# Decoder layer with retrieved experts: low halves of weights on VectorE, scores evicted together with their maximum, one-hots of 16 tokens, retrieval by heads, two u loads ahead of the gates' load

## The chip, the cores and the metric

The program runs on one core of a Trainium2 chip, in one launch. The metric is the device time of one execution in microseconds (us). The core has a matrix engine (TensorE, PE in the profile, with its weight loads as PEld), VectorE (DVE), ScalarE (ACT), GpSimd (POOL) and a queue that issues most DMAs (SP). Every engine works through its own instructions in a fixed order and waits on semaphores for the others.

## The reference

One layer over 16 meta tokens and 512 tokens of width 1024; float32 in and out.

```python
h = layer_norm(concat([meta, x]))
q, k, v, gb, gc, z = split(h @ w_in)                 # w_in: 1024 x 3072
attn = softmax(q1 k1 / 8 + bias) v - lam * softmax(q2 k2 / 8 + bias) v   # 4 heads, causal, T5 bias
conv = gb * short_conv(gc * z)                       # width 3, causal
h = layer_norm(ALPHA * h + concat([norm(attn), conv]) @ w_out)
# PEER: 8 heads, 2 x 128 sub-keys, 16384 experts
s = (h @ w_q) . sub_keys                             # per token: 8 heads x 2 x 128 scores
s1, i1 = top16(s[..., 0, :]); s2, i2 = top16(s[..., 1, :])
sc, ci = top16(s1[:, None] + s2[None, :])
idx = i1[ci // 16] * 128 + i2[ci % 16]; g = softmax(sc)
out = sum over the 128 experts of a token:  g * gelu(h . u[idx]) * v[idx]
return layer_norm(ALPHA * h + out)[16:]
```

## The kernel before

Float32 operands are split into a float16 high half (made by ScalarE) and a low half (made by VectorE), and each product is three float16 matmuls (`mm3`, line 145). `split` (line 105) does that for u and v rows, for projections and for most weights. `load_w` loads one block of 512 weight columns in four pieces `w` (four buffers) and splits them into `wh` and `wl`, of which there are three buffers. For the blocks gc, z, gb and w_out two of the four pieces go through `split_pool`, in which ScalarE scales the piece in place and rounds it, and GpSimd makes the low half.

The code is written in the order of the layer, and a scheduler of the tile framework fixes the order of each engine's instructions from it, within the limits of the tile buffers.

1. Up to about 320 us: layer norm, projections, and 16 attention units (4 blocks of 128 queries `i`, 4 heads `h`). `att_a` multiplies queries with keys, VectorE evicts the two score tiles with scale and bias (L348), takes the row maximum over both (L352), and ScalarE takes the exponential. `att_t`, `att_b` and `att_c` transpose, multiply with v and normalise; `rstd` does the reciprocal square root on GpSimd. Convolution and output projection (`conv_gc` and the others) are put between the units.
2. About 320 to 440 us: queries of the retrieval (`pq_mm`), scores with the sub-keys, and `top16` on VectorE, in four rounds of two heads; a round multiplies the queries of both its heads, then their scores, then ranks them.
3. About 440 to 717 us: 56 u blocks (of 128 that cover all experts) are multiplied with the tokens of blocks 1 to 3 by `u_first`; the first `NSP` results go to memory (`ascr`), the other `NR` stay on the chip. Between them the generator `finish_topk` is advanced by a budget (`SIDE` per block against the numbers it yields): it ranks the candidates of a block of tokens, retrieves expert numbers by a comparison and a multiplication (`soh`, L598 to L604), and, for blocks 1 to 3, builds for `TB` tokens at a time one-hot tiles (L664 to L667), which TensorE multiplies to a gate matrix (`expand`). The matrices go through memory: GpSimd's queue writes `gscr`, SP's queue loads `gr`.
4. From 717 us: for each of the 128 blocks a product gate times activation `w` (L821) and 18 matmuls with v (L831). The 72 blocks that are left get their u product one step ahead (`prep`). Token block 0 is served by 128 gathers (`g_issue`, `g_dot`, `g_acc`) in VectorE's spare time.

Of the kernel before, what the change touches and what calls it, by code (L numbers as in the profile page):

```python
# [16 lines left out]
P = 128  # L17
# [22 lines left out]
TB = 8  # L40
# [3 lines left out]
NSP = 36  # L44
NR = 20
# [7 lines left out]
def build(tc, A, out):  # L53
# [72 lines left out]
    def split_pool(hi, lo, src, scale):  # L126
        S.activation(src, src, AF.Copy, scale=scale)
        S.activation(hi, src, AF.Copy)
        G.tensor_tensor(lo, src, hi, op=OP.subtract)

    def load_w(src, nb, pool=False):
        wh = wst.tile([P, KT, 512], F16, name="wh")
        wl = wst.tile([P, KT, 512], F16, name="wl")
        for j in range(4):
            w = wst.tile([P, 2, 512], F32, name="w", bufs=4)
            s = slice(j * 2, j * 2 + 2)
            SY.dma_start(w, src[nb, :, s, :])
            (split_pool if pool and j % 2 else split)(wh[:, s, :], wl[:, s, :], w, WS)
        return wh, wl
# [17 lines left out]
    with ExitStack() as s1:  # L157
# [92 lines left out]
        for c0, c1 in ((0, 512), (512, RW)):  # L250
            p = bank()
            PE.matmul(p[:H, :c1 - c0], rb, oh[:, c0:c1], start=True, stop=True)
            S.copy(row[:, c0:c1], p[:H, :c1 - c0])
# [34 lines left out]
        def conv_gc(c):  # L288
            if c == 0:
                W["gc"] = load_w(A["w_in"], 4, True)  # L290
# [3 lines left out]
        def conv_z(c):  # L294
            if c == 0:
                W["z"] = load_w(A["w_in"], 5, True)
# [4 lines left out]
        def conv_gb(c):  # L301
            if c == 0:
                W["gb"] = load_w(A["w_in"], 3, True)
# [8 lines left out]
        def out_proj(i, nb):  # L312
            for b in range(2):
                if ("wo", b) not in W:
                    W["wo", b] = load_w(A["w_out"], b, True)
# [19 lines left out]
        def att_a(i, h):  # L335
# [3 lines left out]
            qs = slice(i * P, (i + 1) * P)  # L339
            rs_ = [slice(m * DK, (m + 1) * DK) for m in range(2)]  # L340
# [173 lines left out]

    with ExitStack() as s5:
# [7 lines left out]
        for nb in range(4):  # L523
            if nb < 3:
                wqs[nb + 1] = load_w(A["w_q"], nb + 1)
            w = wqs.pop(nb)
            if nb == 0:
                pq = pq0
            else:
                pq = [None] * 4  # L530
                pq_mm(w, pq, 0, 512)
            todo = []
            for hh in range(2):
                h = nb * 2 + hh
                pqh = kp.tile([P, 2, T], F16, name="pqh", bufs=2)
                pql = kp.tile([P, 2, T], F16, name="pql", bufs=2)
                for j in range(2):
                    split(pqh[:, j, :], pql[:, j, :], pq[2 * hh + j], 1.0 / WS)
                for i in range(NT):
                    ts = slice(i * P, (i + 1) * P)  # L540
                    p = bankA()
                    for j in range(2):
                        mm3(p[:, j * NK:(j + 1) * NK], lambda k: pqh[:, j, ts], lambda k: pql[:, j, ts],
                            lambda k: keyh[:, h, j, :], lambda k: keyl[:, h, j, :], 1)
                    sc = kp.tile([P, 2, NK], F32, name="sc", bufs=8)
                    S.activation(sc, p[:, :2 * NK].rearrange("p (j n) -> p j n", j=2), AF.Copy,
                                 scale=1.0 / WS)
                    todo.append((h, i, sc))
            for n, (h, i, sc) in enumerate(todo):
                if nb == 3 and n % 3 == 0:  # L550
                    u_first(n // 3)
# [351 lines left out]
```

## Time and profile before

| | |
|---|---|
| median of 3 runs | 1530.44 us (1519.59 to 1531.7) |
| profiled execution | 1525.47 us; span of the trace 1523.7 us |
| mean granted TensorE clock | 0.968 |
| busy: PE, DVE, ACT, POOL | 92%, 80%, 48%, 20% of the span |
| DMA | 370.90 MB, 243 GB/s over the span |

The times are those of whole executions. The profile is of one execution; its span begins with the first instruction, so the 1.8 us between its two numbers lie around the span. A busy share is an average over the four stages, which have different limits.

### The profile page before, as it was taken

Reading aid. Unit: us, or ns where it says so; the run is one execution under the profiler, and the core shown is the slowest. Engines: PE = TensorE matmul, PEld = TensorE weight load, DVE = VectorE, ACT = ScalarE, POOL = GpSimd, SP = SyncE. Lnnn points to the kernel's source line nnn. Section 1 sums busy time; section 2 is a strip of 40 time slices with the busy share of each in tenths; the row PEclk is TensorE's granted clock in tenths of the full one; section 3 lists DMA queues with packets and bytes.
Section 4 is the critical chain, followed back from the end, with each engine's and each line's share of the span. In section 5 each row is a group of like instructions: output and inputs, shape, how many; then the busy total and the mean of one; then the engine's idle time right before and its main releaser. Section 6 shows DMA issues by size and latency. Waiting matters only on the chain.

```text
span 1523.7 us, 22893 instructions
## 1 busy us (share of the span) xinstructions
PE 1399.8 (92%) x8656; PEld 760.9 (50%) x8656; DVE 1224.3 (80%) x2375; ACT 730.2 (48%) x1243; POOL 299.8 (20%) x288
## 2 busy tenths in 40 slices
PE   6889897889989889897999999999999999999993
PEld 2345455554546556573554545545454545554551
DVE  8454687479999999894797897878978797888785
ACT  5364455351337658484454444444445444444441
POOL 2031111110001313011123232212212222212214
PEclk9989998989999999998999999999999999999997
DMA  6452110060055848589898998989989999999851
GB/s 231 146 176 76 57 56 1 30 208 15 2 171 180 262 140 272 186 237 365 333 365 337 355 378 337 374 341 338 403 319 360 357 348 352 362 352 366 298 197 56
DMA packets 85987, 370.90 MB, mean 243 GB/s; under 512 B 10495, under 2 KB 15647, under 8 KB 69492
## 3 DMA queue, kind: packets, MB, share of 16 engines
q1 hardware_dynamic: 57724, 200.53, 36.0%
q0 software_dynamic: 28144, 168.90, 30.1%
q8 instruction: 67, 1.10, 0.3%
q14 instruction: 44, 0.36, 0.1%
q10 hardware_dynamic: 8, 0.01, 0.0%
HBM read 335.05 MB, written 35.69 MB: 243 GB/s over the span
## 4 chain that ended last, share of the span: by engine, by line
PE 46%; issue 19%; DVE 19%; DMA 6%; POOL 6%; ACT 3%; POOLq 0%; SPq 0%; DVEq 0%; ACTq 0%
PE po L831 21%; PE pa L145 12%; PE b L145 11%; POOL grow L686 3%; DMA grow<-peer_uv,idx 2%; DVE ul L107 2%; DVE wl L107 1%; DMA gscr<-stg 1%; DVE rh L666 1%; DVE rl L667 1%; DVE oh L664 1%; DMA w<-w_in 1%; DVE oh L665 1%; DMA kf<-keysT 1%; POOL ry L83 1%
## 5 line engine op out<-in xcount | busy, mean ns | idle before, releaser
L145 PE MATMUL pa<-tTh,uh 128*128 128x384 f16 x1024 | 336.0, 328 | 10.3 <-ACT act L499 9.9
L145 PE MATMUL pa<-tTh,ul 128*128 128x384 f16 x1024 | 335.8, 328 | 9.0 <-DVE ul L107 9.0
L145 PE MATMUL pa<-tTl,uh 128*128 128x384 f16 x1024 | 335.9, 328 | 0.0
L686 POOL DMA_INDIRECT grow<-peer_uv,idx x128 | 169.9, 1328 | 615.8 <-DVE acc L703 552.4
L145 PEld LDWEIGHTS <-uh 128*128 128x128 f16 x2048 | 200.2, 98 | 148.4 <-issue 13.9
L831 PEld LDWEIGHTS <-wwh 128*128 128x128 f16 x1488 | 145.8, 98 | 181.2 <-ACT wwh L823 12.0
L107 DVE SCALAR_TENSOR_TENSOR ul<-uf,uh 128x1024 f16<-128x1024 f32 x128 | 161.5, 1262 | 90.9 <-ACT uh L106 90.9
L106 ACT ACTIVATE uh<-uf 128x1024 f16<-128x1024 f32 x128 | 135.2, 1056 | 198.1 <-PE pa L145 192.3
L831 PE MATMUL po<-pvh,wwh 128*128 128x512 f16 x744 | 182.1, 381 | 10.9 <-ACT pvh L106 10.4
L831 PE MATMUL po<-pvl,wwh 128*128 128x512 f16 x744 | 181.8, 381 | 0.0
L831 PE MATMUL po<-pvh,wwl 128*128 128x512 f16 x744 | 180.8, 379 | 0.0
L107 DVE SCALAR_TENSOR_TENSOR pvl<-vf,pvh 128x1024 f16<-128x1024 f32 x128 | 155.6, 1219 | 26.4 <-ACT pvh L106 26.4
L106 ACT ACTIVATE pvh<-vf 128x1024 f16<-128x1024 f32 x128 | 134.3, 1050 | 70.4 <-PE po L831 70.2
L703 DVE SCALAR_TENSOR_TENSOR acc<-grow,gact,acc 128x1024 f32<-128x1024 f32 x127 | 162.5, 1279 | 0.6 <-ACT gact L695 0.6
L693 DVE SCALAR_TENSOR_TENSOR grow<-grow,x 128x1024 f32<-128x1024 f32 x128 | 156.1, 1219 | 7.6 <-DMA grow<-peer_uv,idx 7.4
L145 PEld LDWEIGHTS <-ul 128*128 128x128 f16 x1024 | 100.8, 98 | 78.0 <-DVE ul L107 11.4
L823 ACT ACTIVATE wwh<-w 128x384 f16<-128x384 f32 x128 | 66.7, 522 | 145.3 <-DVE w L821 145.3
L145 PE MATMUL b<-tTh,wh 128*128 128x512 f16 (+4 forms) x416 | 123.6, 322 | 0.9 <-ACT tTh L124 0.9
L145 PE MATMUL b<-tTl,wh 128*128 128x512 f16 (+4 forms) x416 | 124.0, 320 | 0.0
L145 PE MATMUL b<-tTh,wl 128*128 128x512 f16 (+4 forms) x416 | 123.8, 320 | 0.0
L831 PEld LDWEIGHTS <-wwl 128*128 128x128 f16 x744 | 72.8, 98 | 87.8 <-issue 0.2
L145 PEld LDWEIGHTS <-wh 128*128 128x128 f16 x832 | 70.3, 100 | 63.7 <-issue 4.3
(229 smaller groups left out, 1911.3 us busy)
## 6 DMA issues: line engine op xcount, KB each, us to landing
uf<-uT SPq DMA_DIRECT2D x128, 512.0 KB, 6.5
vf<-vL SPq DMA_DIRECT2D x128, 512.0 KB, 7.3
gscr<-stg POOLq DMA_DIRECT2D x12, 2048.0 KB, 12.4
gr<-gscr SPq DMA_DIRECT2D x32, 768.0 KB, 8.1
w<-w_in SPq DMA_DIRECT2D x24, 512.0 KB, 4.8
w<-w_q SPq DMA_DIRECT2D x16, 512.0 KB, 4.1
ascr<-act POOLq DMA_DIRECT2D x18, 384.0 KB, 4.8
aload<-ascr SPq DMA_DIRECT2D x18, 384.0 KB, 8.9
```

Of the source, the lines that this page charges most:

```text
L83: G.tensor_tensor(y[:n], ve[:n], mhalf[:n].to_broadcast([n, w]), op=OP.pow)
L106: S.activation(hi, src, AF.Copy, scale=scale)
L107: V.scalar_tensor_tensor(lo, src, scale, hi, op0=OP.mult, op1=OP.subtract)
L145: m = PE.matmul(o, a(k), b(k), start=first and n == 0, stop=last and n == 3 * nk - 1)
L664: V.tensor_tensor(pairs(o2), row, mid(gT[:, 1, ts]), op=OP.is_equal)
L665: V.tensor_tensor(pairs(o1), row, mid(gT[:, 0, ts]), op=OP.is_equal)
L666: V.tensor_tensor(pairs(rh), pairs(o2), mid(gT[:, 2, ts]), op=OP.mult)
L686: G.indirect_dma_start(out=uv, out_offset=None, in_=A["peer_uv"], in_offset=bass.IndirectOffsetOnAxis(ap=idx[:, j:j + 1], axis=0))
L693: V.scalar_tensor_tensor(uv[:, :D], uv[:, :D], 1.0, x1[0], op0=OP.mult, op1=OP.mult, accum_out=c)
L703: V.scalar_tensor_tensor(acc, uv[:, D:], c, acc, op0=OP.mult, op1=OP.add)
L823: S.activation(wh, w, AF.Copy)
L831: PE.matmul(po[i][c], x[:, ts], y[:, c * 512:(c + 1) * 512], start=f and k == 0, stop=False)
```

## The change

- `split_pool` is gone: all pieces of all weights go through `split`.
- `att_a` evicts a score tile with one instruction that also keeps the running minimum of the negated score. The bias is stored eight times larger, the exponential gets the scale -1, and the separate maximum is gone.
- The retrieval's queries, scores and ranking run in eight rounds of one head; the queries of the next head are multiplied ahead of the scores of the present one. The three u products among them stand at other places.
- In `finish_topk` the expert numbers are stored in pairs, the multiplication of the retrieval reads them in pairs, and all eight of them run on VectorE (four ran on GpSimd).
- One-hots are built for 16 tokens at a time, in two buffers (three before), and expanded one group behind (two before).
- 40 of the 56 early u results go to memory (36 before), 16 stay (20 before). The u loads and splits of the first two later blocks are written ahead of the first load of gates.

```diff
-TB = 8
+TB = 16
-NSP = 36
-NR = 20
+NSP = 40
+NR = 16
...
-            (split_pool if pool and j % 2 else split)(wh[:, s, :], wl[:, s, :], w, WS)
+            split(wh[:, s, :], wl[:, s, :], w, WS)
...
-                    V.scalar_tensor_tensor(lg[:, m, f0:f1], p[:, :f1 - f0], DK ** -0.5,
-                                           bias[h][:, c0 + f0:c0 + f1], op0=OP.mult, op1=OP.add)
-            nm = small.tile([P, 2], F32, name="nm")
+                    V.tensor_tensor_reduce(lg[:, m, f0:f1], p[:, :f1 - f0], bias[h][:, c0 + f0:c0 + f1],
+                                           scale=-DK ** -0.5, scalar=nm[:, m:m + 1] if f0 else 3.0e38,
+                                           op0=OP.add, op1=OP.min, accum_out=nm[:, m:m + 1])
-            V.tensor_reduce(nm, lg[:, :, :w], axis=AX.X, op=OP.max, negate=True)
             for m in range(2):
                 S.activation(lg[:, m, :w], lg[:, m, :w], AF.Exp, bias=nm[:, m:m + 1],
-                             accum_out=z[:, m:m + 1])
+                             scale=-1.0, accum_out=z[:, m:m + 1])
...
+        def pq_head(h):
+            nb, hh = divmod(h, 2)
+            if hh == 0 and nb < 3:
                 wqs[nb + 1] = load_w(A["w_q"], nb + 1)
             if nb == 0:
+                return pq0[2 * hh:2 * hh + 2]
+            pq = [None] * 4
+            pq_mm(wqs[nb], pq, 0, 512, (2 * hh, 2 * hh + 1))
+            return pq[2 * hh:2 * hh + 2]
+
+        nxt = pq_head(0)
+        for h in range(PH):
+            pq = nxt
...
+            if h + 1 < PH:
+                nxt = pq_head(h + 1)
...
-        V.tensor_copy(ivh, iv[i])
+        for j in range(2):
+            V.tensor_copy(ivh[:, j], iv[i][:, :, j, :].unsqueeze(3).to_broadcast([P, PH, K, 2]))
...
-            (V if i <= 1 else G).tensor_tensor(
-                o, o, ivh[:, :, j, :].unsqueeze(3).to_broadcast([P, PH, K, K]), op=OP.mult)
+            o2 = o.rearrange("p h a (m e) -> p (h a) m e", e=2)
+            V.tensor_tensor(o2, o2, ivh[:, j].rearrange("p h a e -> p (h a) e").unsqueeze(2)
+                            .to_broadcast([P, PH * K, K // 2, 2]), op=OP.mult)
...
-                o1 = tkp.tile([P, TB, NK], F16, name="oh1", bufs=3)
-                o2 = tkp.tile([P, TB, NK], F16, name="oh2", bufs=2)
-                rh = tkp.tile([P, TB, NK], F16, name="rh", bufs=3)
-                rl = tkp.tile([P, TB, NK], F16, name="rl", bufs=3)
+                o1 = tkp.tile([P, TB, NK], F16, name="oh1", bufs=2)
+                o2 = tkp.tile([P, TB, NK], F16, name="oh2")
+                rh = tkp.tile([P, TB, NK], F16, name="rh", bufs=2)
+                rl = tkp.tile([P, TB, NK], F16, name="rl", bufs=2)
...
-                yield 1.8
-                if len(prev) == 2:
+                yield 3.2
+                if len(prev) == 1:
                     flush()
...
+    for n1 in [n for n in seq if n >= NSP + NR][:2]:
+        u_load(n1)
     load_g(0)
```

The scheduler's order changes in two places that matter below. The first is VectorE ahead of the first attention scores, about 100 us into the program (`wl` are low halves of weights, `ql` of the query projection, `lg` the evicted scores, `nm` their extremum). Before:

```order
L107 SCALAR_TENSOR_TENSOR wl<-w,wh 128x1024 x2
L107 SCALAR_TENSOR_TENSOR ql<-b,qh 128x512
L107 SCALAR_TENSOR_TENSOR wl<-w,wh 128x1024
L107 SCALAR_TENSOR_TENSOR ql<-b,qh 128x512 x3
L348 SCALAR_TENSOR_TENSOR lg<-pa,bias_92 128x144 x2
L107 SCALAR_TENSOR_TENSOR wl<-w,wh 128x1024
L352 TENSOR_REDUCE nm<-lg 128x2
```

VectorE at the same place in the changed kernel:

```order
L107 SCALAR_TENSOR_TENSOR wl<-w,wh 128x1024 x4
L107 SCALAR_TENSOR_TENSOR ql<-b,qh 128x512
L107 SCALAR_TENSOR_TENSOR wl<-w,wh 128x1024 x3
L107 SCALAR_TENSOR_TENSOR ql<-b,qh 128x512 x2
L107 SCALAR_TENSOR_TENSOR wl<-w,wh 128x1024
L107 SCALAR_TENSOR_TENSOR ql<-b,qh 128x512
L107 SCALAR_TENSOR_TENSOR wl<-w,wh 128x1024 x3
L345 ISA lg,nm<-pa,bias_92 128x144
L345 ISA nm 128x1
```

Counted from the program's start, 16 low halves of weights stood on VectorE ahead of the first scores, and now 24 do, the four of block gb among them; the eviction is an instruction and a second one that stores `nm`.

The second place is ScalarE from the eviction of the last gate matrices (`stg`) to the first gated activation of the last stage (`wwh`), with the u blocks' high halves (`uh`) and products (`act`). Before:

```order
L645 COPY stg<-b 128x4x128 x6
L106 ACTIVATE uh<-uf 128x1024
L499 ACTIVATE act<-pa 128x384
...
L499 ACTIVATE act<-pa 128x384
L823 ACTIVATE wwh<-w 128x384
L106 ACTIVATE pvh<-vf 128x1024
L823 ACTIVATE wwh<-w 128x384 x2
L106 ACTIVATE uh<-uf 128x1024
L499 ACTIVATE act<-pa 128x384
```

ScalarE at the same place in the changed kernel:

```order
L649 COPY stg<-b 128x4x128 x8
L106 ACTIVATE uh<-uf 128x1024
L495 ACTIVATE act<-pa 128x384
...
L495 ACTIVATE act<-pa 128x384
L829 ACTIVATE wwh<-w 128x384
L106 ACTIVATE pvh<-vf 128x1024
L829 ACTIVATE wwh<-w 128x384 x2
L106 ACTIVATE uh<-uf 128x1024
L495 ACTIVATE act<-pa 128x384
```

The rows read alike, but their numbers differ: before, all 56 early products `act` stand ahead of the first `wwh`, now 51 do. On TensorE the last group of one-hots is multiplied behind u product 51 of 56 before and behind product 46 now, and VectorE has 52 low halves `ul` ahead of its last one-hot before and 48 now; ahead of its first `w` it has 57 before and 52 now.

## Rows read from the trace of the kernel before

**Rows 1.** Windows: us, busy us (instructions) of PE, PEld, DVE, ACT, POOL, clock, DMA share, GB/s
```profile
160.00:320.00 160.00, 133.15 (x1024) 81.19 (x1023) 110.81 (x197) 76.36 (x162) 26.62 (x50) 0.89 0.19 59
440.00:687.00 247.00, 223.63 (x1831) 148.29 (x1830) 237.71 (x538) 162.03 (x200) 47.80 (x30) 0.97 0.66 212
717.60:1503.00 785.40, 781.41 (x4032) 394.37 (x4031) 664.69 (x857) 359.96 (x655) 173.90 (x144) 1.00 0.88 337
```

**Rows 2.** Groups by line, VectorE, 100 to 300 us: busy us, mean ns, idle before
```profile
L348 DVE SCALAR_TENSOR_TENSOR lg<-pa,bias 128x144 f32<-128x144 f32 (+3 forms) x32 | 14.9, 494 | 0.0
L352 DVE TENSOR_REDUCE nm<-lg 128x2 f32<-128x288 f32 (+3 forms) x16 | 13.5, 843 | 0.0
```

**Rows 3.** Line 693, a VectorE instruction that also writes out its accumulator: ns min/median/max
```profile
L693 DVE DVE_READ_ACCUMULATOR grow<-grow,x x128: 74/83/86, 739.3 to 1479.5; 128x1 f32 x128
```

**Rows 4.** Timeline of GpSimd and VectorE around the first `rstd` of the attention (start, us)
```profile
163.68 2.13 POOL L129 TENSOR_TENSOR wl<-w,wh 128x1024 f16<-128x1024 f32 x1 [19.57 <-DVE wl L107]
...
168.45 2.98 DVE L407 SCALAR_TENSOR_TENSOR o<-o,ry,sg 128x128 f32<-128x128 f32 x4 [2.88 <-POOL ry L87]
...
206.21 1.14 DVE L407 SCALAR_TENSOR_TENSOR o<-o,ry,sg 128x128 f32<-128x128 f32 x4 [1.47 <-POOL ry L87]
```

**Rows 5.** Timeline of TensorE and VectorE at the first scores
```profile
99.37 0.38 PE L145 MATMUL b<-tTh,wl 128*128 128x512 f16 x1
...
103.39 0.51 DVE L348 SCALAR_TENSOR_TENSOR lg<-pa,bias 128x144 f32<-128x144 f32 x2
```

**Rows 6.** Waits of VectorE, 340 to 440 us: us in total, times, longest
```profile
DVE pql L107 <- ACT pqh L106: 4.9, 2, 2.7
```

**Rows 7.** Timeline of GpSimd and VectorE around the multiplications of the retrieval
```profile
516.43 3.63 POOL L600 TENSOR_TENSOR soh<-soh,ivh 128x2048 f16<-128x2048 f16 x1 [11.39 <-DVE soh L598]
...
516.46 3.76 DVE L567 TENSOR_TENSOR cand<-svt 128x128 f32<-128x128 f32 x1
...
528.92 3.03 DVE L107 SCALAR_TENSOR_TENSOR ul<-uf,uh 128x1024 f16<-128x1024 f32 x1
...
544.02 0.24 DVE L567 TENSOR_TENSOR cand<-svt 128x128 f32<-128x128 f32 x1
544.18 4.68 DVE L107 SCALAR_TENSOR_TENSOR ul<-uf,uh 128x1024 f16<-128x1024 f32 x1
...
599.89 0.69 DVE L603 TENSOR_TENSOR soh<-soh 128x1024 f16<-128x1024 f16 x1 [3.54 <-POOL soh L600]
```

**Rows 8.** VectorE in the third stage: timeline, then the group of line 600
```profile
515.12 1.23 DVE L598 TENSOR_TENSOR soh<-ab,i 128x2048 f16<-128x2048 f16 x1
516.26 0.28 DVE L610 TENSOR_REDUCE tz<-td 128x8 f32<-128x128 f32 x1
...
639.86 0.69 DVE L667 TENSOR_TENSOR rl<-oh,gT 128x1024 f16<-128x1024 f16 x1
640.46 0.68 DVE L664 TENSOR_TENSOR oh<-iot,gT 128x1024 f16<-128x1024 f16 x1
...
L600 DVE TENSOR_TENSOR soh<-soh,ivh 128x2048 f16<-128x2048 f16 x4 | 9.1, 2283 | 0.0
```

**Rows 9.** From the last one-hot to the last stage: timelines and the chain (start, us)
```profile
685.92 0.68 DVE L667 TENSOR_TENSOR rl<-oh,gT 128x1024 f16<-128x1024 f16 x1
686.52 1.22 DVE L107 SCALAR_TENSOR_TENSOR ul<-uf,uh 128x1024 f16<-128x1024 f32 x1
...
692.16 17.74 DMA gscr<-stg
...
710.17 5.08 DMA gr<-gscr
...
717.63 2.72 PE L831 MATMUL po<-pvh,wwh 128*128 128x512 f16 x6 [10.45 <-ACT pvh L106]
...
731.63 3.90 PE pa L145 x24
```

**Rows 10.** DMA issues of the gates in the page: KB each, median us to landing
```profile
gscr<-stg POOLq DMA_DIRECT2D x12, 2048.0 KB, 12.4
```

More of the change, by code (lines that the diff above doesn't have):

```diff
@@ L124, in rows_to_T, with load_w @@
             (S.copy if d is tTh and not dve else V.tensor_copy)(d[:, :, c0:c0 + n], p[:, :, :n])
[L126 to L131, printed above, removed]
+    def load_w(src, nb):
         wh = wst.tile([P, KT, 512], F16, name="wh")
@@ L252, in build @@
             PE.matmul(p[:H, :c1 - c0], rb, oh[:, c0:c1], start=True, stop=True)
-            S.copy(row[:, c0:c1], p[:H, :c1 - c0])
+            S.activation(row[:, c0:c1], p[:H, :c1 - c0], AF.Copy, scale=DK ** 0.5)
         drow = dram.tile([H, RW], F32, name="drow")
@@ L289, in conv_gc @@
             if c == 0:
-                W["gc"] = load_w(A["w_in"], 4, True)
+                W["gc"] = load_w(A["w_in"], 4)
             S.activation(gc[:, c, :2], projT(W["gc"], c, NM - 2, NM), AF.Copy, scale=1.0 / WS)
@@ L295, in conv_z @@
             if c == 0:
-                W["z"] = load_w(A["w_in"], 5, True)
+                W["z"] = load_w(A["w_in"], 5)
             for s, r0, r1 in ((slice(0, 2), NM - 2, NM), (slice(2, 2 + T), NM, L)):
@@ L302, in conv_gb @@
             if c == 0:
-                W["gb"] = load_w(A["w_in"], 3, True)
+                W["gb"] = load_w(A["w_in"], 3)
             y = wk.tile([P, T], F32, name="y", bufs=1)
@@ L314, in out_proj @@
                 if ("wo", b) not in W:
-                    W["wo", b] = load_w(A["w_out"], b, True)
+                    W["wo", b] = load_w(A["w_out"], b)
             p = bank()
@@ L339, in att_a @@
             qs = slice(i * P, (i + 1) * P)
+            nm = small.tile([P, 2], F32, name="nm")
             rs_ = [slice(m * DK, (m + 1) * DK) for m in range(2)]
@@ L513, in u_first @@
                 G.dma_start(ascr[n1 - 1:n1 + 1].rearrange("n p t -> p n t"), apair[0])
+    FIRST = []
     with ExitStack() as s5:
@@ L522, in build @@
             split(keyh[:, 2 * hf:2 * hf + 2], keyl[:, 2 * hf:2 * hf + 2], kf, WS)
-        for nb in range(4):
-            if nb < 3:
+        def pq_head(h):
+            nb, hh = divmod(h, 2)
+            if hh == 0 and nb < 3:
                 wqs[nb + 1] = load_w(A["w_q"], nb + 1)
-            w = wqs.pop(nb)
             if nb == 0:
[L528 to L531, printed above, removed]
+                return pq0[2 * hh:2 * hh + 2]
+            pq = [None] * 4
+            pq_mm(wqs[nb], pq, 0, 512, (2 * hh, 2 * hh + 1))
+            return pq[2 * hh:2 * hh + 2]
@@ L532, in build @@
+        nxt = pq_head(0)
+        for h in range(PH):
+            pq = nxt
+            pqh = kp.tile([P, 2, T], F16, name="pqh", bufs=2)
+            pql = kp.tile([P, 2, T], F16, name="pql", bufs=2)
+            for j in range(2):
+                split(pqh[:, j, :], pql[:, j, :], pq[j], 1.0 / WS)
+            if h + 1 < PH:
+                nxt = pq_head(h + 1)
             todo = []
[L533 to L536, printed above, removed]
+            for i in range(NT):
+                ts = slice(i * P, (i + 1) * P)
+                p = bankA()
@@ L537, in build @@
                 for j in range(2):
[L538 to L548, printed above, removed]
@@ L549, in build @@
-            for n, (h, i, sc) in enumerate(todo):
-                if nb == 3 and n % 3 == 0:
-                    u_first(n // 3)
+                    mm3(p[:, j * NK:(j + 1) * NK], lambda k: pqh[:, j, ts], lambda k: pql[:, j, ts],
+                        lambda k: keyh[:, h, j, :], lambda k: keyl[:, h, j, :], 1)
+                sc = kp.tile([P, 2, NK], F32, name="sc", bufs=8)
+                S.activation(sc, p[:, :2 * NK].rearrange("p (j n) -> p j n", j=2), AF.Copy,
+                             scale=1.0 / WS)
@@ L552, in build @@
+                todo.append((i, sc))
+            for n, (i, sc) in enumerate(todo):
+                if (h, n) in ((6, 0), (6, 3), (7, 2)):
+                    u_first(len(FIRST))
+                    FIRST.append(0)
                 s2 = kp.tile([P, 2, NK], F32, name="s2", bufs=2)
@@ L591, in finish_topk @@
         V.tensor_tensor(ab[:, 0], f[0], f[2], op=OP.add)
-        ivh = tkp.tile([P, PH, 2, K], F16, name="ivh")
-        V.tensor_copy(ivh, iv[i])
+        ivh = tkp.tile([P, 2, PH, K, 2], F16, name="ivh")
+        for j in range(2):
+            V.tensor_copy(ivh[:, j], iv[i][:, :, j, :].unsqueeze(3).to_broadcast([P, PH, K, 2]))
         yield 2.0
```

## The prediction

> **What bounds the kernel now.** I read the busy windows first, since the share over the whole span mixes stages. In the last stage TensorE is busy 781.4 of 785.4 us at full clock [rows 1]: that stage costs what its matmuls cost, and the change leaves it 128 gated blocks and 72 u products, the same numbers. What moves the end is therefore when the last stage starts. In the third stage VectorE is busy 237.7 of 247 us, more than TensorE with 223.6 [rows 1], so there VectorE sets the pace. The second stage hangs on VectorE as well: its one wait is 4.9 us for the queries' high halves [rows 6]. In attention nobody is full: TensorE 133 of 160 us, VectorE 111 [rows 1]; there a chain that goes back and forth between VectorE, ScalarE and GpSimd decides. Between the third and the last stage lies the gates' round trip through memory: from the end of the last one-hot (686.60) to the first matmul with v (717.63) pass 31.0 us, for which TensorE has five u products and then idles 10.45 us [rows 9].
>
> **The change part by part. Weights and scores.** Ten low halves come to VectorE at 1.22 us, the length of such an instruction that nothing disturbs [rows 9]; that is +12.2 us. The 16 maxima go, -13.5 us [rows 2]. The new eviction isn't in the trace. Its nearest rows are the old eviction, 0.49 us in the mean [rows 2], and the second instruction that stores an accumulator, 0.083 us [rows 3]; 40 of these make +3.3 us. The 40 evictions themselves could cost twice the old ones (+15 us for the 32 in rows 2), or the same; below the same I see no reason for, as they read the same operands. I take the same, since the instruction of line 693 is a fused one too. VectorE's total so hardly moves (+2.0 us); what counts is where the pieces lie.
>
> Ahead of the first scores the order puts 24 low halves where 16 stood. The last four, of block gb, need buffers that the query projection reads until 99.75 [rows 5]. From there, one piece on ScalarE (taken as long as VectorE's), four on VectorE at 1.22 and the last query's low half put the first scores near 106.5 instead of 103.39 [rows 5]: +3 us. The maximum that is gone from there gives part back; I take +1.5, ends 0 and +4.
>
> At the first `rstd` of the attention GpSimd first made a weight's low half, 2.13 us, and the four scalings of `o` behind it took 2.98 us beside another one, against 1.14 us when undisturbed [rows 4]. Both go: -4.0. But the order puts two more low halves between these scalings and the transposes that wait for them, +2.4. Net -1.5, ends -4 and +2.
>
> In the rest of attention the maxima of 11 units go (11 of the 13.5 us, as the later units are the wider), the stores of `nm` cost 2.5 and two more low halves stand there (2.4): 6 us off VectorE. It is busy 69% of that stage and each maximum is a link between eviction and exponential, so some passes through: I take -4, ends 0 and -6. ScalarE loses ten instructions, which nobody waited for in total; I give them nothing. Attention in sum: **-4**, ends -10 and +6.
>
> **Retrieval by heads.** TensorE multiplies the same; queries of a head now come between two heads' scores, so the two waits of 4.9 us [rows 6] have other work in front of them. VectorE is behind TensorE there, so what it doesn't wait it gains. It can't gain more than the 4.9 and it might wait eight short times instead of two longer ones: **-4.5**, ends 0 and -5.
>
> **Third stage.** Four multiplications leave GpSimd. While they ran, VectorE's instructions with two inputs stood still: an addition took 3.76 us instead of 0.24, low halves of u took 4.68 and 3.03 instead of 1.22, and once VectorE waited 3.54 us for the result [rows 7]. Together 3.5 + 3.5 + 1.8 + 3.5 = 12.3 us. They return to VectorE as four instructions of 1.14 us from start to start, if the paired reading runs as fast as the comparison of the same size does, and the four that were there fall from 2.28 to that [rows 8]: +0.3 in sum. If paired reading gained nothing, they would cost 2.28 each, +9.1. The comparison and the one-hots read in pairs already at the fast rate, so I stay with +0.3, and add 1 for four more small casts. One-hots: 192 instructions become 96 of double length. From start to start a small one takes 0.60 and a double one 1.14 [rows 8], which saves 96 x 0.06 = 5.8 us.
>
> The durations of the same rows say more: 2 x 0.69 - 1.23 is 0.15 us of fixed part, so 14.4 us for 96. A row of the timeline, however, begins before the one ahead has ended, and starts are what a full engine is paid by. [...]
>
> Ahead of its last one-hot VectorE has 48 low halves of u instead of 52: -4.9. Together -12.3 + 0.3 + 1 - 5.8 - 4.9 = -21.7 us. VectorE also idled 9.3 us in this stage [rows 1], of which 3.5 are counted; of the rest I take back 2.5. The last one-hot is 24 us nearer to the start of the stage.
>
> That isn't the gain. Behind the last expansion now stand ten u products instead of five. ScalarE and VectorE are in order and wait there for the gates with 51 products and 52 low halves done, so TensorE gets only to product 52 under the round trip: six products of 3.90 us [rows 9] where it had five, and its idle time falls from 10.45 to about 6.5 us. Four products, 15.6 us, come after the gates and before the first matmul with v. So: **-24 + 15.6 = -8.5**. The round trip I leave at 31.0: the write of the gates took 17.74 us beside gathers [rows 9], its median is 12.4 [rows 10], and now one gather instead of two stands in front of it, which would give up to -5; as many for the other direction, since three more gathers and u loads still share it. With the idle time not taken back, the stage's ends are -16 and +2, and +11 with slow paired reading.
>
> The four results more that go through memory and back, and the two u loads, are 1.6 MB and 1 MB in a stage whose DMA engines have 0.88 of their time taken, beside full TensorE [rows 1]; nothing, unless that cover goes: at its 337 GB/s they would cost 8 us.
>
> **Sum.** -4 - 4.5 - 8.5 = -17 us on the profiled 1525.5, 1508.5, which is a ratio of 0.9889. The median of the runs shown is 1530.4, 0.3% above the profiled run, so on it I forecast 1513.
>
> **The rivals.** *Gain given back.* The third stage is faster but the products behind the gates and the late first scores take it: attention at 0 or +4, the retrieval waits as before, the third stage at -6. That is -6 to -2, near 1526. For it speaks that TensorE's total work is unchanged and that it idles only 23 of the 247 us [rows 1]. This is also what a fused eviction at twice the price would give.
>
> *Blocks in lockstep, slower.* With two buffers for a one-hot block of 16 tokens, VectorE may only start a block when TensorE has expanded the one two before. VectorE needs 4 x 1.14 + 1.22 = 5.8 us per block [rows 8, 9], TensorE one product of 3.90 and the expansion. If TensorE comes half a product late each time, VectorE waits 1.95 us in each of 24 blocks: +47, 1560. From 0.7 us per block on, the change gains nothing; from 1.4 us it is slower by 1%. Against it: TensorE waits for VectorE in that stage, not the other way.
>
> *The whole fixed part is saved.* If each one-hot that goes takes its 0.15 us along, 14.4 instead of 5.8: 1504. [...]
>
> *The change doesn't do what it says:* the new order still lets VectorE wait for each head's queries, and the fused eviction waits where the maximum did. Then only the third stage counts, 1522.
>
> **How the numbers follow.** Forecast 0.49, gain given back 0.28, lockstep 0.08, whole fixed part 0.06, not as said 0.09. A measurement here tells 1% (15 us) from no change: below 1515 is faster, above 1546 slower. The forecast's own spread of some 10 us leaves a sixth of it within 1%; against that the low ends of the unlikely cases reach below 1515. Faster 0.53, within 1% 0.39, slower 0.08. The range goes from the whole fixed part together with attention's low end (1504 less 6) to a gain given back in full: 1498 to 1530.
>
> **What would show it.** In the changed profile: no VectorE row of 3 us or more between 440 and 690 us; the last one-hot 28 to 36 us earlier; TensorE's idle time behind the last expansion 6 to 7 us instead of 10.45, and four u products between it and the first matmul with v; evictions of 0.49 us in the mean with stores of 0.08; first scores near 106 us; a last stage of 785 us. I am wrong if the new eviction takes over 0.8 us, if rows of line 604 take 2.2 us, or if VectorE waits for TensorE's expansions.

## The result, and the profile after

The changed kernel takes 1516.82 us (median of 20 runs, 1507.73 to 1520.62), the kernel before 1530.39 (20 runs, 1519.59 to 1535.77): a ratio of 0.9913 with an interval of 0.9895 to 0.9931, or 13.6 us less. The forecast was 0.9889 and 1513. The profiled execution took 1515.41 us, with a span of 1513.2.

The windows of the changed kernel, cut at its own places (attention; third stage to the end of the last one-hot; from there to the first matmul with v; from there to the first eviction of an output). Columns as in [rows 1].

```profile
160.00:320.00 160.00, 134.27 (x1016) 78.28 (x1014) 102.77 (x218) 75.56 (x161) 23.39 (x48) 0.91 0.16 53
440.00:657.11 217.11, 203.38 (x1696) 136.10 (x1694) 216.29 (x439) 154.52 (x189) 30.51 (x28) 0.97 0.73 230
657.11:708.49 51.38, 44.91 (x271) 27.20 (x272) 22.78 (x31) 23.22 (x32) 5.70 (x4) 0.90 1.00 381
708.49:1482.30 773.81, 770.66 (x3988) 389.77 (x3986) 651.53 (x835) 353.61 (x647) 182.19 (x131) 1.00 0.88 336
```

VectorE is still full in the third stage (216.3 of 217.1 us), but its last one-hot ends at 657.11 instead of 686.60 [rows 9]: 29.5 us earlier. From there to the first matmul with v it takes 51.4 us instead of 31.0, so that 9 us are left: the matmuls with v start at 708.49 instead of 717.63. In attention VectorE is 8 us less busy than in [rows 1], TensorE as busy as before. The chain of the changed kernel behind the last one-hot (start, us):

```profile
662.43 15.94 DMA gscr<-stg
...
678.58 6.68 DMA gr<-gscr
...
690.53 18.12 PE pa L140 x96
708.66 3.45 PE po L837 x16
```

Write and load of the gates take 22.6 us (22.8 in [rows 9]), and then come the four u products (96 matmuls) that the forecast spoke of. They take 18.1 us instead of 15.6, and TensorE had idled ahead of them, as these windows show: idle from 684 to 690.5, and the granted clock at 0.87 in the stretch behind, where in `e9_all_behind`, without the idle time, it is 1.00.

```profile
662.00:684.00 22.00, 22.00 (x137) 13.21 (x135) 3.68 (x3) 5.74 (x8) 4.63 (x3) 1.00 1.02 387
684.00:690.50 6.50, 0.13 (x1) 0.00 (x0) 5.09 (x8) 3.84 (x6) 0.00 (x0) 0.85 0.89 339
690.50:708.66 18.16, 18.13 (x97) 10.23 (x97) 10.64 (x11) 9.02 (x13) 0.00 (x0) 0.87 1.01 390
```

What TensorE waits for from 440 to 710 us (us in total, times, longest): the 10.45 us for `pvh` of [rows 9] have become 6.4 us for an `act`.

```profile
PE pa L140 <- ACT act L495: 12.3, 3, 6.4
PE b L647 <- DVE rl L671: 2.8, 5, 0.9
```

The groups of VectorE that are new, by form (busy us, mean ns; attention, then the third stage): the fused eviction lasts as long as the old one did (685 ns against 684 at 512 columns), its store 84 ns, and the multiplication that reads in pairs costs 1.22 us, like the comparison.

```profile
L345 DVE CUSTOM_DVE_ANT_0 lg<-pa,bias 128x512 f32<-128x512 f32 x8 | 5.2, 685 | 0.0
...
L345 DVE DVE_READ_ACCUMULATOR2_ANT nm<- 128x1 f32 x40 | 3.4, 84 | 0.0
...
L671 DVE TENSOR_TENSOR rl<-oh,gT 128x2048 f16<-128x2048 f16 x24 | 29.5, 1227 | 0.0
...
L604 DVE TENSOR_TENSOR soh<-soh,ivh 128x2048 f16<-128x2048 f16 x8 | 9.8, 1221 | 0.0
```

One thing in the pair of profiles misleads. The first scores are evicted at 110.53 us, against 103.39 [rows 5] and some 106 in the forecast. Most of this isn't the change: in the window from 40 to 50 us TensorE was granted a clock of 1.00 before and 0.66 after, at nearly the same work. The window of before, then of the changed kernel:

```profile
40.00:50.00 10.00, 9.58 (x48) 3.97 (x49) 8.63 (x15) 5.55 (x9) 2.33 (x6) 1.00 0.84 280
```

```profile
40.00:50.00 10.00, 9.21 (x33) 3.40 (x34) 8.74 (x14) 4.24 (x6) 1.09 (x2) 0.66 0.81 279
```

The experiment `e5_mult_alone`, whose code up to there is that of before, has 0.66 as well, and `e2_tb8`, whose code up to there is that of the changed kernel, has 1.00. The first eviction of a score in the changed kernel, then in `e2_tb8`:

```profile
110.53 0.30 DVE L345 CUSTOM_DVE_ANT_0 lg<-pa,bias 128x144 f32<-128x144 f32 x1
```

```profile
106.12 0.30 DVE L345 CUSTOM_DVE_ANT_0 lg<-pa,bias 128x144 f32<-128x144 f32 x1
```

So at an equal clock the first scores come 2.7 us later than before, as forecast (+3), and the profile of before had a start that is some 4 to 6 us better than that of the twelve kernels with the lower clock. For the experiments I therefore count from a later mark that it doesn't touch: the end of the last `MAX8` on a retrieval score, which closes the second stage (423.8 us before, 424.2 after).

### The profile page after: what moved, and what is told of

Its sections match the earlier page's. It is cut to its first block, busy times and chain, and to the rows that moved or that the text cites. A ratio compares the mean times of both kernels' runs of the same rounds, so it can differ in the third digit from the quotient of the medians.

```text
span 1513.2 us, 22819 instructions
## 1 busy us (share of the span) xinstructions
PE 1405.9 (93%) x8656; PEld 761.6 (50%) x8656; DVE 1204.2 (80%) x2321; ACT 717.5 (47%) x1233; POOL 273.2 (18%) x276
## 4 chain that ended last, share of the span: by engine, by line
PE 58%; issue 16%; DVE 12%; POOL 5%; DMA 5%; ACT 3%; POOLq 0%; SPq 0%; DVEq 0%; ACTq 0%
PE po L837 25%; PE pa L140 18%; PE b L140 13%; DMA grow<-peer_uv,idx 2%; DVE wl L107 1%; POOL gscr L657 1%; DMA gscr<-stg 1%; DVE ul L107 1%; DVE acc L707 1%; POOL grow L690 1%; POOL ry L83 1%; DVE iv L149 1%; DVE s L147 1%; DVE iv L146 1%; POOL ascr L509 1%
## 5 line engine op out<-in xcount | busy, mean ns | idle before, releaser
L140 PE MATMUL pa<-tTh,uh 128*128 128x384 f16 x1024 | 338.0, 330 | 12.5 <-ACT act L495 12.3
L690 POOL DMA_INDIRECT grow<-peer_uv,idx x128 | 182.4, 1425 | 609.8 <-DVE acc L707 525.8
L107 DVE SCALAR_TENSOR_TENSOR ul<-uf,uh 128x1024 f16<-128x1024 f32 x128 | 156.4, 1223 | 92.8 <-ACT uh L106 92.8
```

The source lines that it names most:

```text
L107: V.scalar_tensor_tensor(lo, src, scale, hi, op0=OP.mult, op1=OP.subtract)
L140: m = PE.matmul(o, a(k), b(k), start=first and n == 0, stop=last and n == 3 * nk - 1)
L690: G.indirect_dma_start(out=uv, out_offset=None, in_=A["peer_uv"], in_offset=bass.IndirectOffsetOnAxis(ap=idx[:, j:j + 1], axis=0))
```

## The experiments

All times are set against the kernel before, run on the same chip. "Third stage" runs from the mark to the first matmul with v, "rest" from the mark to the end of the span, both in the one profiled execution; one such number carries 2 us of chance and more: the second stage alone, from the last output projection to the mark, takes from 115.8 to 119.4 us in nine kernels with the same code for it.

| kernel | median us | ratio | interval | third stage | rest |
|---|---|---|---|---|---|
| before | 1530.39 | 1 | | 293.9 | 1099.9 |
| changed | 1516.82 | 0.9913 | 0.9895 to 0.9931 | 284.3 | 1089.0 |
| `e1_two_heads` | 1518.85 | 0.9921 | 0.9894 to 0.9948 | 288.0 | 1089.9 |
| `e2_tb8` | 1510.20 | 0.9891 | 0.9869 to 0.9913 | 281.0 | 1084.3 |
| `e3_pool_mult` | 1529.73 | 0.9999 | 0.9984 to 1.0015 | 297.1 | 1101.2 |
| `e4_old_attention` | 1516.49 | 0.9909 | 0.9886 to 0.9931 | 284.5 | 1088.0 |
| `e5_mult_alone` | 1512.50 | 0.9892 | 0.9868 to 0.9917 | 277.9 | 1084.3 |
| `e6_mult_unpaired` | 1522.76 | 0.9957 | 0.9940 to 0.9974 | 285.7 | 1091.9 |
| `e7_acts_ahead` | 1516.84 | 0.9905 | 0.9877 to 0.9933 | 284.0 | 1084.8 |
| `e8_seven_behind` | 1515.26 | 0.9906 | 0.9886 to 0.9926 | 286.0 | 1086.0 |
| `e9_all_behind` | 1508.56 | 0.9865 | 0.9844 to 0.9886 | 278.1 | 1078.7 |
| `e10_eight_tokens_order` | 1514.32 | 0.9895 | 0.9870 to 0.9919 | 283.6 | 1088.2 |
| `e11_mult_and_sixteen` | 1518.69 | 0.9911 | 0.9883 to 0.9938 | 286.9 | 1095.2 |
| `e12_eight_behind` | 1507.50 | 0.9849 | 0.9824 to 0.9875 | 277.9 | 1078.3 |

My theory was that of the forecast: three terms (attention, retrieval by heads, third stage) that add up. The rivals were that one part carries all of it, or that TensorE's idle time takes up what VectorE saves.

**Parts undone, four kernels made from the changed one.**

`e1_two_heads`: the rounds of the kernel before.

```diff
-        nxt = pq_head(0)
-        for h in range(PH):
...
+        for nb in range(4):
...
+                pq_mm(w, pq, 0, 512)
```

> The changed kernel with the retrieval's queries and scores again in four rounds of two heads. Theory A (the terms add up): VectorE's last score ranking comes 4 to 5 us later than in the changed kernel, everything behind it is moved by as much, and the time is 4 to 5 us above the changed kernel, a ratio to the kernel before of about 0.994. Rival B (TensorE's idle time further on absorbs it): the last one-hot is later but the matmuls with v start at the same place, ratio 0.991.

The ratio is 0.9921, 0.0008 or 1.2 us above the changed kernel. The two intervals overlap almost whole, so 4 to 5 us is at the edge of what they allow. The profiles don't settle it either: the mark comes 3.8 us later than in the changed kernel, but the first scores are already 1.1 us late there, and the third stage behind the mark, whose code the edit leaves alone, is 3.7 us longer too.

`e2_tb8`: one-hots of 8 tokens.

```diff
-TB = 16
+TB = 8
...
-                yield 3.2
-                if len(prev) == 1:
+                yield 1.8
+                if len(prev) == 2:
```

> The changed kernel with one-hots of 8 tokens, the old buffers, two groups behind and the old budget. Theory A (starts count): 96 more instructions cost VectorE 5.8 us, the time is 4 to 6 us above the changed kernel, ratio 0.994 to 0.995. Rival B (durations count, the whole fixed part): 14 us, ratio 1.000. Rival C (the stage is TensorE's by now): the gates are later, but five products instead of ten stand behind them, so TensorE's idle time is the same and so is the time, ratio 0.991.

None of the three: with 8 tokens the kernel comes out faster than with 16, by 3.4 us going by the ratios, whose intervals overlap, and by 4.7 us in the rest of the profile. Its VectorE does have more to do (busy for 245.1 us from the mark to its last one-hot against 232.1, four more low halves of u among it), and the last one-hot ends 12 us later, though its mark comes 6 us earlier, but then five products stand behind it and not ten. Its windows from the mark to the last one-hot and from there to the matmuls with v, and the first of these for the changed kernel:

```profile
418.00:669.43 251.43, 233.77 (x1891) 153.91 (x1889) 245.14 (x636) 166.71 (x206) 33.27 (x31) 0.97 0.68 219
669.42:698.95 29.53, 20.51 (x135) 12.60 (x136) 8.11 (x11) 9.89 (x14) 5.20 (x3) 0.94 0.99 360
```

```profile
424.18:657.12 232.94, 214.49 (x1755) 142.23 (x1753) 232.06 (x528) 158.29 (x195) 31.96 (x30) 0.96 0.70 223
```

`e3_pool_mult`: two pairs of multiplications back on GpSimd.

```diff
-            V.tensor_tensor(o2, o2, ivh[:, j].rearrange("p h a e -> p (h a) e").unsqueeze(2)
+            (V if i <= 1 else G).tensor_tensor(o2, o2, ivh[:, j].rearrange("p h a e -> p (h a) e").unsqueeze(2)
```

> The changed kernel with the two multiplications of the retrieval for token blocks 2 and 3 back on GpSimd, paired reading kept. Theory A: the stretched VectorE instructions return (rows of 3 us and more), 9 to 12 us of VectorE's time, of which TensorE's idle time takes some: 5 to 10 us above the changed kernel, ratio 0.9945 to 0.998. Rival B: TensorE's work hides them, ratio 0.991 to 0.992.

The whole gain is gone: 0.9999, more than either theory had. In its timeline the stretched instructions are back. VectorE around the two first and the two last multiplications, then GpSimd's own rows:

```profile
521.15 4.84 DVE L107 SCALAR_TENSOR_TENSOR ul<-uf,uh 128x1024 f16<-128x1024 f32 x1 [0.24 <-ACT uh L106]
...
592.77 3.50 DVE L573 TENSOR_TENSOR cand<-svt 128x64 f32<-128x64 f32 x1
```

```profile
521.21 3.69 POOL L604 TENSOR_TENSOR soh<-soh,ivh 128x2048 f16<-128x2048 f16 x1
...
592.08 4.11 POOL L604 TENSOR_TENSOR soh<-soh,ivh 128x2048 f16<-128x2048 f16 x1 [5.63 <-DVE soh L601]
```

An addition of 64 elements takes 3.50 us; it took 0.22 in the changed kernel. The low half takes 3.6 us more than its 1.22, and VectorE waits 5.5 us for the products: 12.4 us together, and the third stage is 12.8 us longer. Both stretched instructions have two inputs, and they end 1.1 and 0.1 us behind the multiplication. The forecast let all instructions with two inputs stand still, but beside GpSimd's fourth multiplication in the kernel before (from 592.96 us, 6.89 us long) four of them take 0.67 and 1.21 us, their usual lengths.

`e4_old_attention`: splits by GpSimd and the old eviction.

```diff
-                    V.tensor_tensor_reduce(lg[:, m, f0:f1], p[:, :f1 - f0], bias[h][:, c0 + f0:c0 + f1],
...
+                    V.scalar_tensor_tensor(lg[:, m, f0:f1], p[:, :f1 - f0], DK ** -0.5,
+                                           bias[h][:, c0 + f0:c0 + f1], op0=OP.mult, op1=OP.add)
...
+            V.tensor_reduce(nm, lg[:, :, :w], axis=AX.X, op=OP.max, negate=True)
...
-            split(wh[:, s, :], wl[:, s, :], w, WS)
+            (split_pool if pool and j % 2 else split)(wh[:, s, :], wl[:, s, :], w, WS)
```

> The changed kernel with the splits by GpSimd and the old eviction with its separate maximum. Theory A (what the traces show, the first scores later and nothing won after them): the same time or up to 2 us less than the changed kernel, ratio 0.990 to 0.9915. Rival B (the prediction's term, the profiled run being late by the clock at 40 us alone): 4 us above the changed kernel, ratio 0.994.

0.9909: the same time, as theory A had it. The attention part of the change is worth nothing that can be measured; the interval ends at 0.9931, and the forecast's 4 us would have been 0.994.

**Parts alone, from the kernel before.** After these four the theory of three terms was no longer mine: the multiplications seemed to carry the whole gain, and 16 tokens to cost some of it.

`e5_mult_alone`: only the pairs and the engine.

```diff
+        ivh = tkp.tile([P, 2, PH, K, 2], F16, name="ivh")
...
-            (V if i <= 1 else G).tensor_tensor(
-                o, o, ivh[:, :, j, :].unsqueeze(3).to_broadcast([P, PH, K, K]), op=OP.mult)
+            V.tensor_tensor(o2, o2, ivh[:, j].rearrange("p h a e -> p (h a) e").unsqueeze(2)
+                            .to_broadcast([P, PH * K, K // 2, 2]), op=OP.mult)
```

> The kernel before with one part of the change: expert numbers in pairs and all eight multiplications of the retrieval on VectorE. Theory A (GpSimd's collisions are nearly the whole gain): 10 to 14 us less than before, ratio 0.991 to 0.9935, and the stretch from the last score ranking to the first matmul with v goes from 293.9 us to about 281. Rival B (the gain is spread over the parts, as the prediction's sum has it): 5 us or less, ratio 0.997 or more.

0.9892, 16.5 us less than before: this one part gives all that the whole change gives (0.9913) and perhaps a little more. Its third stage is 277.9 us; the last one-hot ends 11.8 us earlier than before although the mark comes 2 us later, and the stretch behind it is 29.0 us, with five products as before. Its windows from the mark to the last one-hot and from there to the matmuls with v, and the first of these for the kernel before:

```profile
425.95:674.78 248.83, 230.51 (x1894) 152.84 (x1892) 246.21 (x637) 167.41 (x206) 31.82 (x29) 0.99 0.69 221
674.78:703.76 28.98, 20.51 (x136) 12.60 (x136) 8.11 (x10) 9.94 (x14) 5.22 (x3) 0.94 0.98 358
```

```profile
423.75:686.61 262.86, 234.86 (x1894) 154.54 (x1892) 253.54 (x626) 167.21 (x206) 49.26 (x32) 0.97 0.65 208
```

Of the 14.0 us by which the stretch to the last one-hot is shorter, 7.3 are less work for VectorE and 6.7 less idle time.

`e6_mult_unpaired`: only the engine.

```diff
-            (V if i <= 1 else G).tensor_tensor(
+            V.tensor_tensor(
```

> The kernel before with all eight multiplications on VectorE, but the expert numbers read one by one as before. Theory A: four more multiplications of 2.3 us come to VectorE and four stay so long, 9 us of work beside 12 us of stalls that go: a gain of 3 to 6 us, ratio 0.996 to 0.998. Rival (VectorE's time in this stage is worth nothing by itself, only the stalls are): as much as with pairs, ratio 0.991 to 0.9935.

0.9957, 6.6 us less than before, just above what theory A had. The eight multiplications cost VectorE 18.3 us (by form), against 9.7 in `e5_mult_alone`; those 8.6 us are 9.9 us of time by the ratios and 7.8 us of the third stage. So a microsecond of VectorE in this stage is worth about one, when it isn't bought with another order.

```profile
L600 DVE TENSOR_TENSOR soh<-soh,ivh 128x2048 f16<-128x2048 f16 x8 | 18.3, 2285 | 0.0
```

`e11_mult_and_sixteen`: `e5_mult_alone` and the blocks of 16 tokens.

```diff
-TB = 8
-NSP = 36
-NR = 20
+TB = 16
+NSP = 40
+NR = 16
...
-                yield 1.8
-                if len(prev) == 2:
+                yield 3.2
+                if len(prev) == 1:
```

> The kernel before with two parts of the change: the multiplications on VectorE with paired reading, and one-hots of 16 tokens with the numbers 40 and 16 that make room for them. Theory A (what 16 tokens save on VectorE is paid back, since ten products stand behind the last expansion): 3 to 6 us above the kernel before with the multiplications alone (0.9892), ratio 0.991 to 0.993, and 4 to 5 us more from the last score ranking to the end. Rival (the blocks of 16 tokens are a gain of their own, and the changed kernel loses elsewhere): ratio 0.986 to 0.989.

0.9911, the ratio of the changed kernel, and 2.9 us above the multiplications alone; its rest is 11 us longer, more than theory A had, but the profiled execution was the slowest of its six, 3.2 us above their median. In both pairs (this one, and `e2_tb8` against the changed kernel) 16 tokens come out slower, by 2.9 and 3.4 us in the ratios. The intervals of each pair overlap, so that a loss by 16 tokens is likely, not proved; a gain of several microseconds fits neither pair.

**What the ten products behind the last expansion cost.** If it is TensorE's idle time under the round trip and the low clock behind it, another order should give it back.

`e7_acts_ahead`: the changed kernel, with ScalarE's first `wwh` behind the last early `act`, and VectorE's first `w` behind its last `ul`.

```diff
+    la, ll = lasta[0].ins, lastl[0].ins
...
-        mv = V.tensor_tensor(w.rearrange("p (c t) -> p c t", t=CT), a.rearrange("p (c t) -> p c t", t=CT),
...
+        with tc.issue_after(ll):
+            mv = V.tensor_tensor(w.rearrange("p (c t) -> p c t", t=CT), a.rearrange("p (c t) -> p c t", t=CT),
...
-        S.activation(wh, w, AF.Copy)
+        with tc.issue_after(la):
+            S.activation(wh, w, AF.Copy)
```

> The changed kernel with an order: ScalarE's first gated activation waits behind the last of the 56 early u products' activations, and VectorE's first gate product behind their last low half. Theory A (TensorE's idle 6.4 us under the gates' round trip and the slow clock behind it are what the ten products cost): TensorE runs all ten products in one piece, idles 2 us ahead of the matmuls with v, and the time is 4 to 7 us below the changed kernel, ratio 0.987 to 0.989. Rival (gates, loads and first products of the last stage are only moved behind and TensorE waits as long there): ratio 0.991.

0.9905 against 0.9913, nothing to speak of: the rival, but in another form than I wrote. TensorE still waits once for an `act`, 6.7 us. The rows show why, ScalarE's and then the issues on SP's queue. The order I wrote left the high halves of the v blocks free to go ahead, and one stood in front of the activations and waited 10.8 us for a load that SP issues behind the gates' load.

```profile
681.32 0.47 ACT L497 ACTIVATE act<-pa 128x384 f32<-128x384 f32 x1
692.58 1.06 ACT L106 ACTIVATE pvh<-vf 128x1024 f16<-128x1024 f32 x1 [10.79 <-DMA vf<-vL]
```

```profile
684.50 0.33 SPq L798 DMA_DIRECT2D gr<-gscr  x1
684.88 0.43 SPq L824 DMA_DIRECT2D vf<-vL  x1
```

`e8_seven_behind`: that order, and 3.6 for 3.2 in the budget.

```diff
-                yield 3.2
+                yield 3.6
```

> The same order, and a block of 16 tokens is booked with 3.6 instead of 3.2, so that seven u products instead of ten stand behind the last expansion. Theory A: seven products of 3.90 us just cover the 28 us from the last one-hot to the first gate product; the last one-hot comes 4 to 8 us later than in the changed kernel, the matmuls with v start 8 to 12 us earlier, ratio 0.984 to 0.987. Rival (TensorE is full by then ahead of the last one-hot, so that three products there cost as much as they do behind): as with the order alone, ratio 0.987 to 0.989.

0.9906, no gain; the same v block stands in ScalarE's way, for 13.3 us here, and TensorE idles 9.3 us behind the last one-hot. So it says nothing on the number of products.

`e9_all_behind`: as `e7_acts_ahead`, with the v block's split behind the activations too.

```diff
-        with tc.issue_after(la):
+        with tc.issue_after(la), tc.issue_after(ll):
             S.activation(wh, w, AF.Copy)
-        split(vh, vl, vf, WS)
+            split(vh, vl, vf, WS)
```

> The order of the earlier run with all activations ahead, and the halves of the v blocks behind them as well, since there ScalarE waited 10.8 us for a v block whose load stood behind the gates' load in SP's queue. Theory A (only that wait kept the order from working): TensorE has no wait of 6 us for an activation any more, runs ten products in one piece and idles 2 to 4 us ahead of the matmuls with v; from the last score ranking to the end 1084.5 less 4 to 7 us, ratio 0.986 to 0.988. Rival (the v blocks are split later now and TensorE waits for them instead): TensorE's idle time only moves, ratio 0.990 to 0.9915.

0.9865, 7 to 8 us below the changed kernel (0.9913), with intervals that don't overlap, and inside theory A. That fits the idle time (6.4 us) and the low clock behind it (2.5 us) as what the order cost. TensorE is busy 43.5 of 44.0 us from the last one-hot to the matmuls with v, at full clock:

```profile
661.69:705.71 44.02, 43.50 (x287) 26.80 (x288) 17.04 (x24) 19.57 (x28) 5.71 (x4) 1.00 1.02 390
```

The first gate product is made at 693.06, 8 us later than in the changed kernel, and its `wwh` only at 704.20; that costs nothing, since TensorE has other work until then.

`e10_eight_tokens_order`: `e9_all_behind` with 8 tokens and seven products behind.

```diff
-TB = 16
+TB = 8
...
-                yield 3.2
-                if len(prev) == 1:
+                yield 1.65
+                if len(prev) == 2:
```

> That order with one-hots of 8 tokens, two groups behind, a group booked with 1.65, so that seven u products stand behind the last expansion. Theory A (the time is TensorE's work plus its idle time; the 8.5 to 10 us of idle time under the round trip shrink to some 3): 5 to 8 us below the changed kernel with one-hots of 8 tokens, ratio 0.983 to 0.987. Rival (its VectorE has 4 us more to do ahead of the last one-hot and that costs as much): ratio 0.988 to 0.990.

0.9895, the rival's number for another reason: ScalarE waits once more ahead of the last activation, this time for a u block whose load SP issues behind the gates' load, and TensorE idles 6.4 us.

```profile
706.99 1.06 ACT L106 ACTIVATE uh<-uf 128x1024 f16<-128x1024 f32 x1 [8.74 <-DMA uf<-uT]
```

`e12_eight_behind`: `e9_all_behind` with 3.4 in the budget, a third u load ahead, and the gates' load behind it in SP's queue.

```diff
-    for n1 in [n for n in seq if n >= NSP + NR][:2]:
+    for n1 in [n for n in seq if n >= NSP + NR][:3]:
         u_load(n1)
-    load_g(0)
+    with tc.issue_after(lastd[0].ins):
+        load_g(0)
...
-                yield 3.2
+                yield 3.4
```

> The order of the run with everything behind the activations, a block booked with 3.4 so that eight products stand behind the last expansion, a third u load ahead and the gates' load behind it in SP's queue (in the run with seven products ScalarE waited 8.7 us for a u block whose load stood behind the gates'). Theory A (TensorE's idle time under the round trip is already gone with ten products, so fewer behind only move work): within 3 us of that run, ratio 0.985 to 0.988. Rival (a gate product ready earlier lets the last stage start earlier): 5 us or more below it, ratio under 0.9835.

0.9849, and within 3 us of `e9_all_behind` as theory A had it: 1507.50 us, 9 to 10 us below the changed kernel and the best kernel of this study. Between these two nothing is told apart.

## Why the prediction came out right

The time lies 4 us above the forecast and inside its range, but that the sum came out so near is luck in part, since errors of its terms cancel.

- **Third stage, the multiplications: right in kind, too small.** The forecast had 12.3 us of stalls less 1.3 us of work, 11 us. Alone they give 16.5 us of time and 16.0 us of the third stage (293.9 to 277.9); putting four of them back costs 12.8. The stalls are what the rows show; of the 16.5 us the pairs are worth 9.9 and the change of engine by itself 6.6. To the last one-hot VectorE's idle time fell by 6.7 us, where the forecast had 3.5 here and 2.5 for the stage; another 2.0 us came in the stretch behind (31.0 to 29.0), which it left as it was.
- **Third stage, 16 tokens: right in mechanism.** The step that subtracted the u products behind the gates (-5.8 and -4.9 for VectorE, +15.6 for four products) made +4.9 us; measured were 2.9 and 3.4 us in the ratios, 4.7 and 11 us in single profiles. The six products under the round trip, four behind it, and 6.4 us of idle time instead of 10.45 stand in the profile as forecast. The low clock behind the idle time (2.5 us) was not in the sum; the kernel before has one too, but in its last stage, where the granted clock is 0.85 in the first 15 us and 1.00 in the changed kernel. Nor was it in the sum that the first product behind the idle time starts 5.3 us after the gates have landed, with three `wwh`, a `pvh` and a `uh` on ScalarE ahead of the `act` that it waits for; before, the first matmul with v started 2.4 us after them.
- **One-hots, starts or durations.** The forecast priced them by their starts and named the durations, 14.4 us for 96, as the other way. The four groups of durations fall from 130.1 us (192 instructions of `e5_mult_alone`) to 117.7 (96 of the changed kernel), 12.4 us. VectorE's busy time from the mark to the last one-hot falls by 8.1 us in both pairs (`e11_mult_and_sixteen` against `e5_mult_alone`, 246.2 to 233.2, less 4.9 for four low halves of u; the changed kernel against `e2_tb8`, 245.1 to 232.1, alike), and the starts themselves give 6.7 (602 ns from one start to the next before, 1135 now). So the starts were the better price, a little low by the rounding to 0.60 and 1.14. The 14.4 us are not reached by any of these. The saving didn't reach the time, since the order took it.
- **Attention: mis-sized, -4 forecast, about 0 measured.** The old attention in the changed kernel gives the same time. From the first eviction of a score to the end of the last output projection I read 201.2 us in the mean of five kernels with the old attention (200.3 to 203.6) and 197.6 in the mean of nine with the new one (195.4 to 198.4): 3.6 us are gained there, and they go into the first eviction, which comes later by 2.7 us at the full clock (106.12 against 103.39) and by 3.7 at the lower one (111.9 in the mean of eight against 108.1 in the mean of four). The start was forecast well as +3; from there on the forecast had -7 (the -1.5 that it set against the start, -1.5 and -4), twice what came. The durations were forecast well too: VectorE is busy 127.7 instead of 138.2 us from 100 to 320. The step that failed is the size of "some passes through". An engine that is busy 111 of 160 us gives up time that nobody waits for, and TensorE is full for much of it: it is busy all of the 40 us from 120 to 160 in both kernels.
- **Retrieval by heads: mis-sized, -4.5 forecast, about -1.** VectorE's wait for `pqh` fell from 4.9 [rows 6] to 2.0 us, but undoing it costs 1.2 us in the ratio. From the last output projection to the mark, five kernels with rounds of two heads take 118.2 us in the mean (116.6 to 120.1), nine with single heads 117.1 (115.8 to 119.4). The pair of profiles that the forecast would be checked with (120.1 and 115.8) happens to give 4.3.
- **Rivals.** Products given back behind the gates: yes, inside the forecast's own sum. Lockstep of the blocks: no; VectorE waits 0.7 us in all from 440 to 660, and for an `uh`.

So -4, -4.5 and -8.5 were about 0, -1 and -9.6, the last of these -16 for the multiplications and +6 for 16 tokens with what came with it (277.9 to 284.3). Two pairs of medians say the same of the attention, the single heads and the u loads together: `e11_mult_and_sixteen`, which lacks all three, has 0.9911 against 0.9913 for the changed kernel, and `e5_mult_alone`, which has 8 tokens and lacks all three, has 0.9892 against 0.9891 for `e2_tb8` (whose numbers are 40 and 16, not 36 and 20). Whatever these parts give lies within the intervals, 3 to 5 us.

From the first to the last matmul with v the last stage takes 784.1 us against 783.4, the same time, as the forecast had it. To the end of the span it is 1.4 us shorter (804.7 against 806.1), since 20.6 us and not 22.6 pass behind the last of these matmuls. That was not forecast. The u loads are not the reason: this end takes 22.4 to 22.6 us in before, `e5_mult_alone` and `e6_mult_unpaired` and 20.6 to 20.9 in the other eleven, and `e11_mult_and_sixteen`, without u loads ahead, is one of them. What shortens it stays open.

## What to carry to other kernels

Where an elementwise pass on GpSimd runs beside a full VectorE, it can cost more than it would take on VectorE (four multiplications, 1.22 us each there, cost 12.8 us here): look for VectorE rows that take several times their usual length while a GpSimd row lasts (3.50 us instead of 0.22). Time saved on the engine that paces a stage need not be paid out (16 tokens took 8.1 us off VectorE and brought no gain); so follow the saving to TensorE's next wait, and count the products that then stand behind that wait. An order that keeps one wait off an in-order engine must also cover the instructions that may slip in ahead of it, and their loads' places in the DMA queue: three of the five orders tried here failed on a load that stood behind the gates' load.

## What the hardware showed

- TensorE's granted clock between 40 and 50 us was 1.00 in the profiled runs of before and of `e2_tb8`, 0.50 in that of `e3_pool_mult` and 0.66 in the other eleven, at nearly the same work. In all fourteen TensorE idles 2.29 us just ahead of that (from 38.1 us before, from 38.5 in the changed kernel); in twelve the clock then falls to 0.50, in two it does not. The last low half of q is made at 102.8 to 103.5 us in these two and at 107 to 109 in all others. What decides it the records don't show.
- Behind 6.4 us of idle time four u products took 18.1 us at a granted clock of 0.87; without the idle time (`e9_all_behind`) all of them ran at 1.00.
- The two-part eviction (main instruction, store of the extremum) lasts 84 to 91 ns longer than one that only evicts, at every width from 144 to 512 columns: its main instruction is within 7 ns of the old one, its store takes 84 ns.
- A multiplication of 128x2048 float16 elements with an operand repeated along the innermost axis takes 2.28 us on VectorE, and 1.22 us when that operand is stored in pairs and read in pairs (`e6_mult_unpaired`, `e5_mult_alone`).
